# A hybrid decoder layer on one core: later uses of re-read left factors, and four factors of the output product in an earlier pair

## The chip, the cores and the metric

The program runs on one core of a Trainium2 chip. The metric is the device time of one execution in microseconds (us). The unchanged kernel took 1967.01 us as the median of 3 runs (1965.29 to 1967.56). Engines are named as in the profile: PE (TensorE matmul), PEld (its weight loads), DVE (VectorE), ACT (ScalarE), POOL (GpSimd), SP (SyncE, which issues the DMAs).

## The reference

One layer over 512 tokens of width 2048, all in float32: a normalised input projection, two kinds of attention heads side by side, an output projection with residual, and a gated feed-forward part with residual.

```python
h = rms_norm(x, norm1_g)
proj = h @ w_in                                     # 2048 x 6160
qa, ka, va, ra, ga, qb, kb, vb = split(proj)
log_g = log_sigmoid(ga @ gla_gate_w2 + gla_gate_b) / 16
out_a = rms_norm(chunked_gated_linear_attention(qa, ka, va, log_g)) * silu(ra)   # 4 heads
out_b = dilated_attention(rms_norm(qb), rms_norm(kb), vb, rel_bias)              # 8 heads
x = x + concat(out_a, out_b) @ w_out                # 2048 x 2048
h2 = rms_norm(x, norm2_g)
x = x + (silu(h2 @ w_gate) * (h2 @ w_up)) @ w_down  # 2048 x 5632, 5632 x 2048
```

## The kernel before, in words

**Products.** Every large product is done in pairs of 512 output columns. A pair halves the tokens, the contraction rows and the columns, and forms the 2 x 2 block product with seven block products (P1, P5, P6, P3, P7, P2, P4 in this order, line 32) in place of eight. Each of the seven has a left factor made of the activations (A11, S1, S2, S4, S3, A12, A22, line 37) and a right factor that is a quarter of the weights or the difference of two. With A21 for the fourth part, S1 = A21 + A22, S2 = S1 - A11, S4 = A12 - S2 and S3 = A11 - A21. The contraction is cut into four *groups* of 256 rows in each part, so a pair is 28 groups (21 in the last two pairs): group 0 to 3 are P1, 4 to 7 P5, 8 to 11 P6, 12 to 15 P3, 16 to 19 P7, 20 to 23 P2, 24 to 27 P4. "S1 of part 2" below means the factor S1 of the third 256-row cut; it is needed by group 6 of its pair.

**Precision.** Each factor is split in a high and a low float32r part, and a group is twelve 128x512 matmuls: eight with the high part of the weights (`wh`), four with the low part (`wl`).

**The stream.** `stream` (L318) runs over all groups of all pairs. In group k it emits, in this order: `run_soon`; a demand that the left factor of group k+1 exists (`ensure`, which calls `finish`); the ACT cast to `wh` of group k+1 (L331); the DVE difference of the weights of group k+2 where the product has one (L256; P5, P6, P7 and P4 do); the DVE difference that makes `wl` of group k+1 (L335); eight matmuls; a `step` of the background work; four matmuls. `wh` and `wl` have two buffers each.

**Background work.** Everything else is generators in the list `background`. `step(n)` takes n units from the head of the list (a `yield` is one unit unless it says another cost); each pair has its rate of units in a group. `later(units, fn)` runs fn some steps on, `soon(fn, groups)` some groups on, and `finish` draws from the head until a demanded factor is there.

**Left factors.** An activation block that ends a pair is transposed by PE, stored to DRAM (`transposed_store`, L1122), and read back in parts of 256 KB. `Operand.split` (L172) makes a factor of a part: an ACT cast (L174) and a DVE subtraction (L175), and for S1, S2, S4 and S3 a DVE addition or subtraction before (L1251, L1253, L1255 in `late_jobs`; L193 to L200 in `build`; L215 in `early`).

**The order of pairs.** The first pair (q, k of the linear attention) has an order written out by hand. Then follow the other input columns; the **sixth pair** is the gate `ra` (`final_gate`, L1155), under which the last dilated heads run as background. The **seventh and eighth pair** are the output projection, whose left factors (`opm`) come from the DRAM blocks `mix_d`: 4 to 7 from the dilated heads, 0 to 3 from the gate's four results. `final_out` (L1346) adds the residual, stores rows to `x1_d` and, in the eighth pair, writes the scaled and transposed blocks `xn_d` 4 to 7 of the next operand. `first_columns` (L1389) re-reads the rows that the seventh pair stored, scales and transposes them to `xn_d` 0 to 3; it runs in the eighth pair, as do `operand_jobs` (L1285, all factors of parts 0 and 1 of `opn`). The **ninth pair** is the first of eleven feed-forward pairs on `opn`; the last six pairs are the down projection.

**What sets the order on an engine.** The first pair is issued as written. For all the rest a planner in the framework orders each engine's instructions when the program is built. It keeps a simulated clock: the emission order is only a priority, and an instruction goes to its engine as soon as, by that clock, its inputs are there and nothing earlier in emission is ready. The engine then runs the planned order strictly, whatever the real times are.

Of the kernel before, what the change touches and what calls it, by code (L numbers as in the profile page):

```python
# [10 lines left out]
F32 = mybir.dt.float32  # L11
# [7 lines left out]
P = 128  # L19
# [88 lines left out]
def block_kernel(ctx: ExitStack, tc: tile.TileContext, ins, out):  # L108
# [56 lines left out]
    class Operand:  # L165
# [14 lines left out]
        def build(self, g, r11, r21, r12, r22):  # L180

            get = lambda r: r() if callable(r) else r
            tt = nc.vector.tensor_tensor
            r11, r22 = get(r11), get(r22)
            yield
            yield
            self.split("A11", g, r11)
            r21 = get(r21)
            yield
            self.split("A22", g, r22)  # L190
            r12 = get(r12)
            yield
            tt(r22, r21, r22, op=ALU.add)  # L193
            self.split("S1", g, r22)
            yield
            tt(r21, r11, r21, op=ALU.subtract)
            tt(r11, r22, r11, op=ALU.subtract)
            self.split("S2", g, r11)
            yield
            tt(r11, r12, r11, op=ALU.subtract)  # L200
            self.split("S4", g, r11)
            yield
            self.split("S3", g, r21)
            yield
            self.split("A12", g, r12)
            yield

        def early(self, g, r11, r21):

            pair_ = apool.tile([P, 2, 2, 256], F32, name=nm("top"), tag="A")  # L210
            r11, r21 = r11(pair_[:, 0]), r21(pair_[:, 1])
            yield
            self.split("A11", g, r11)
            yield
            nc.vector.tensor_tensor(r21, r11, r21, op=ALU.subtract)  # L215
            self.split("S3", g, r21)
            yield

# [99 lines left out]
    def stream(pairs):  # L318
# [183 lines left out]
    deferred = []  # L502

# [4 lines left out]
    def step(n=1):  # L508
        for d in list(deferred):
            d[0] -= 1  # L510
            if d[0] <= 0:
                deferred.remove(d)
                d[1]()
        if any(d[2] for d in deferred):
            return
        spent, cost = 0.0, 0
        while background and spent + 1e-6 < n:
            if spent:
                run_soon()
            try:  # L520
                cost = next(background[0])
                spent += 1.0 if cost is None else cost
            except StopIteration:
                background.pop(0)
        return spent

    def finish(ready):

        tries = 0
        while not ready():  # L530
            tries += 1
            assert tries < 100
            run_soon()
            try:
                next(background[0])
            except StopIteration:
                background.pop(0)
# [513 lines left out]
    def together(*gens):  # L1051

        gens = list(gens)
        while gens:
            spent = 0.0
            for g in list(gens):
                try:
                    cost = next(g)
                    spent += 1.0 if cost is None else cost
                except StopIteration:  # L1060
                    gens.remove(g)
            yield spent
# [8 lines left out]
    def heads_norm(t, then):  # L1071
# [8 lines left out]
        def rest():  # L1080
# [74 lines left out]
    def final_gate(half, which, tiles, acc_):  # L1155
        og = onorm.pop((half, which))
        if tiles is None:
            tiles = [cpool.tile([P, 512], F32, name=nm("cr"), tag="C") for _ in range(2)]
            src = acc_
        else:  # L1160
            src = tiles
        for m in range(2):
            if src is acc_:
                nc.vector.scalar_tensor_tensor(
                    halves(og[m]), unfolded(src[m]), row_scale(half, m), halves(og[m]),
                    op0=ALU.mult, op1=ALU.mult,
                )
                neg = nrs1[:, 2 * half + m : 2 * half + m + 1]
                nc.scalar.activation(halves(tiles[m]), unfolded(src[m]), AF.Exp, scale=neg)
            else:  # L1170
                nc.vector.tensor_tensor(og[m], src[m], og[m], op=ALU.mult)
                nc.scalar.activation(tiles[m], src[m], AF.Exp, scale=-1.0)
            nc.scalar.activation(tiles[m], tiles[m], AF.Ln, bias=1.0)
            nc.scalar.activation(tiles[m], tiles[m], AF.Exp, scale=-1.0)

        def rest():
# [3 lines left out]
            later(1 + (src is tiles), lambda: transposed_store(  # L1180
# [3 lines left out]
        soon(rest, 2)  # L1184
# [3 lines left out]
    def part(src, half):  # L1188
        def get(t=None):
            assert (id(src), half) in done  # L1190
            if t is None:
                t = rpool.tile([P, 2, 256], F32, name=nm("r"), tag="r")
            load(t, src[:, :, half * 256 : (half + 1) * 256])
            return t

        return get

    def early_jobs(op, groups, tops, flip):

        h0, h1 = (1, 0) if flip else (0, 1)  # L1200
        jobs = [op.early(g, part(tops[g], h0), part(tops[g], h1)) for g in groups]
        next(jobs[0])
        yield
        for i, job in enumerate(jobs):
            if i + 1 < len(jobs):
                next(jobs[i + 1])
# [402 lines left out]
```

## Time and profile before

| | |
|---|---|
| median of 3 runs | 1967.01 us (1965.29 to 1967.56) |
| the profiled execution's own time | 1968.84 us |
| its span, first to last instruction | 1967.1 us |
| PE busy | 1927.6 us (98%) |
| DVE busy | 1653.7 us (84%) |
| ACT busy | 1093.8 us (56%) |
| mean granted TensorE clock | 0.998 |

The busy shares are averages over the whole span. Where stretches are looked at one by one, a row gives the length, then the busy time of PE, PEld, DVE, ACT and POOL with the number of instructions in brackets, the granted clock and the share of the DMA engines. In the lists of waits a row reads: engine and line that waited, what it waited for, then us in total, how often, the longest. In a timeline a row is start, length, engine, line, what is written from what, how many, and in square brackets the idle time just before it with what ended it.

By the first matmul of each group of twelve, the sixth pair runs from 449.6 to 561.0 us, the seventh to 645.5, the eighth to 732.2, the ninth to 813.6 and the tenth to 887.9.

### The profile page before, as it was taken

To read this page: it belongs to the slowest core of one execution; us is meant where nothing else is said; L and a number is where in the kernel's file an instruction comes from. 1 tells how busy PE (TensorE), PEld (TensorE's weight loads), DVE (VectorE), ACT (ScalarE), POOL (GpSimd) and SP (SyncE) were. 2 spreads that over 40 slices of the span, in tenths; PEclk is the share of its full clock that TensorE was granted. 3 is DMA by queue.
4 is the path that set the end of the run, shared out by engine and by line. 5 is a ranking of instruction groups with operands and counts; after the bars stand their busy time and mean duration, and the time that the engine had idled before them with its cause. 6 is when DMAs were issued, how large, how long until landed. Compare 5 with 4: busy or idle time off the path is not lost.

```text
span 1967.1 us, 25785 instructions
## 1 busy us (share of the span) xinstructions
PE 1927.6 (98%) x9226; PEld 1670.9 (85%) x9226; DVE 1653.7 (84%) x1850; ACT 1093.8 (56%) x1600; POOL 60.9 (3%) x81
## 2 busy tenths in 40 slices
PE   8999999999999999999999999999999999999998
PEld 7888888888878877888888888888888888888887
DVE  8997787868789889878878878878879989989987
ACT  8554564566766766545545445545446646546443
POOL 0000230010000000000000000000000000000000
PEclk9999999999999999999999999999999999999999
DMA  8447455463766684554554553554555865855662
GB/s 278 141 162 266 119 171 170 134 200 124 221 213 202 215 288 152 177 167 133 178 170 127 179 163 127 176 164 130 172 163 168 299 203 185 310 183 175 236 214 75
DMA packets 237114, 360.45 MB, mean 183 GB/s; under 512 B 18246, under 2 KB 96783, under 8 KB 236984
## 3 DMA queue, kind: packets, MB, share of 16 engines
q1 hardware_dynamic: 236776, 358.72, 57.6%
q8 instruction: 72, 1.18, 0.3%
q14 instruction: 58, 0.48, 0.1%
q10 hardware_dynamic: 208, 0.08, 0.0%
HBM read 296.59 MB, written 64.51 MB: 184 GB/s over the span
## 4 chain that ended last, share of the span: by engine, by line
PE 75%; DVE 8%; DMA 5%; issue 3%; ACT 2%; POOL 0%; SPq 0%; DVEq 0%; ACTq 0%
PE acc L367 71%; DVE wl L335 3%; DVE wa L256 2%; PE bank L1129 1%; DVE AS L175 1%; PE bank L987 1%; DMA q<-in_x 1%; DMA xn_d<-oT 1%; ACT wh L331 1%; DMA q<-y_d 0%; DVE seed L294 0%; PE bank L1019 0%; DVE seed L1334 0%; DMA r<-xn_d 0%; DMA wc<-in_w_down 0%
## 5 line engine op out<-in xcount | busy, mean ns | idle before, releaser
L367 PE MATMUL acc<-wh,AS 128*128 128x512 f32 x3008 | 712.5, 380 | 0.6 <-ACT wh L331 0.5
L367 PEld LDWEIGHTS acc<-wh,AS 128*128 128x128 f32 x3008 | 569.8, 190 | 82.3 <-ACT wh L331 1.8
L331 ACT CAST wh<-wa 128x1024 fp32r<-128x1024 f32 x376 | 394.0, 1048 | 392.4 <-PE acc L367 363.0
L367 PE MATMUL acc<-wh,AA 128*128 128x512 f32 x2256 | 535.0, 380 | 0.0
L335 DVE TENSOR_TENSOR wl<-wa,wh 128x1024 fp32r<-128x1024 f32 x376 | 456.3, 1217 | 69.2 <-ACT wh L331 43.6
L367 PEld LDWEIGHTS acc<-wh,AA 128*128 128x128 f32 x2256 | 427.4, 190 | 61.4 <-ACT wh L331 0.9
L367 PE MATMUL acc<-wl,AS 128*128 128x512 f32 x1504 | 395.3, 385 | 9.7 <-DVE wl L335 9.5
L367 PEld LDWEIGHTS acc<-wl,AS 128*128 128x128 f32 x1504 | 279.4, 189 | 62.0 <-DVE wl L335 21.0
L367 PE MATMUL acc<-wl,AA 128*128 128x512 f32 x1128 | 298.1, 387 | 7.9 <-DVE wl L335 7.7
L367 PEld LDWEIGHTS acc<-wl,AA 128*128 128x128 f32 x1128 | 209.6, 190 | 41.5 <-DVE wl L335 12.4
L331 ACT CAST wh<-wb 128x1024 fp32r<-128x1024 f32 x94 | 98.5, 1049 | 129.7 <-PE acc L367 127.8
L331 ACT CAST wh<-wc 128x1024 fp32r<-128x1024 f32 x94 | 98.4, 1047 | 111.5 <-PE acc L367 101.7
L331 ACT CAST wh<-wd 128x1024 fp32r<-128x1024 f32 x94 | 98.5, 1048 | 105.8 <-PE acc L367 102.3
L256 DVE TENSOR_TENSOR wa<-wc,wa 128x1024 f32<-128x1024 f32 x94 | 114.4, 1221 | 46.2 <-DMA wc<-in_w_gate 25.1
L335 DVE TENSOR_TENSOR wl<-wc,wh 128x1024 fp32r<-128x1024 f32 x94 | 114.5, 1218 | 35.6 <-ACT wh L331 35.6
L335 DVE TENSOR_TENSOR wl<-wd,wh 128x1024 fp32r<-128x1024 f32 x94 | 114.3, 1219 | 34.9 <-ACT wh L331 28.2
L335 DVE TENSOR_TENSOR wl<-wb,wh 128x1024 fp32r<-128x1024 f32 x94 | 113.6, 1216 | 5.5 <-ACT wh L331 5.5
L256 DVE TENSOR_TENSOR wb<-wd,wb 128x1024 f32<-128x1024 f32 x94 | 114.3, 1216 | 1.1 <-DMA wd<-in_w_in 0.6
L256 DVE TENSOR_TENSOR wa<-wb,wa 128x1024 f32<-128x1024 f32 x94 | 113.6, 1218 | 0.8
L256 DVE TENSOR_TENSOR wa<-wd,wa 128x1024 f32<-128x1024 f32 x94 | 112.8, 1215 | 0.1
L298 DVE SCALAR_TENSOR_TENSOR seed<-acc,rs,seed 128x512 f32<-128x512 f32 x96 | 70.4, 745 | 24.9 <-PE acc L367 24.9
L282 ACT ACTIVATE seed<-acc,rs 128x512 f32<-128x512 f32 x96 | 60.6, 681 | 1.4 <-PE acc L367 0.8
(303 smaller groups left out, 1365.1 us busy)
## 6 DMA issues: line engine op xcount, KB each, us to landing
wa<-in_w_gate SPq DMA_DIRECT2D x44, 512.0 KB, 3.9
wb<-in_w_up SPq DMA_DIRECT2D x44, 512.0 KB, 4.3
wd<-in_w_up SPq DMA_DIRECT2D x44, 512.0 KB, 4.3
wc<-in_w_gate SPq DMA_DIRECT2D x44, 512.0 KB, 3.7
wc<-in_w_in SPq DMA_DIRECT2D x28, 512.0 KB, 3.9
wa<-in_w_in SPq DMA_DIRECT2D x24, 512.0 KB, 5.1
wb<-in_w_in SPq DMA_DIRECT2D x24, 512.0 KB, 6.0
wd<-in_w_in SPq DMA_DIRECT2D x24, 512.0 KB, 5.9
```

The lines of the kernel that those rows point to most:

```text
L175: nc.vector.tensor_tensor(a[:, :, 1, :], src, a[:, :, 0, :].bitcast(F32), op=ALU.subtract)
L256: nc.vector.tensor_tensor(src, self.quarter(one, g), src, op=ALU.subtract)
L282: nc.scalar.activation(halves(t), unfolded(src[m]), AF.Copy, scale=self.scale(half, m))
L298: nc.vector.scalar_tensor_tensor(halves(seed[m]), unfolded(src[m]), self.scale(half, m), halves(seed[m]), op0=ALU.mult, op1=ALU.add,)
L331: nc.scalar.copy(high[k], sources[k])
L335: nc.vector.tensor_tensor(low[k], sources.pop(k), high[k].bitcast(F32), op=ALU.subtract)
L367: nc.tensor.matmul(p.dst[prod][m], a[:, jj, hl, m * P : (m + 1) * P], folded(w[:, jj, :]), start=fresh and g == 0 and len(terms) == 2 and ...
L987: nc.tensor.matmul(lp[:, :n], qh[:, b * P : (b + 1) * P], kh[:, :n], start=True, stop=True)
L1129: nc.tensor.transpose(bk[:, jj, m * P : (m + 1) * P], tiles[m][:, f : f + P], ident)
```

## The change

1. **Three groups between a load and its use.** The stream keeps its group number in `now`. Generators may answer "wait" (`WAIT`, no unit spent), and `step` then asks the next generator in the list. The queue of loaded parts (`staged`) now holds the group of each load, and a use is emitted only when three groups have gone by (`ripe`), unless a factor is demanded (`hurry`). `early_jobs`, `late_jobs`, `operand_jobs` and the loops of `down_jobs` all go through it; `first_columns` waits in the same way between reading rows and scaling them.
2. **Four factors earlier.** S1 and S2 of parts 0 and 1 of `opm` leave the seventh pair's list and become `late_opm[0]`, which runs beside heads 6 and 7 of the dilated attention in the sixth pair, with tiles of its own from the large pool.
3. **The last result of a pair.** `final_gate` first copies the last product out of PSUM with ACT (`emitted`), and does the gate three groups on, where before DVE and ACT read PSUM at once. In the eighth pair's last result the scaling and the transposes come four steps later.
4. `operand_jobs` loads the four parts of part 1 into work tiles (`v`, `T`, `qT`, `kT`) in place of the small pool.

The core of the diff (the removed `build` and `early` are the functions named above):

```diff
@@ stream @@
+            now[0] = k
             run_soon()
             ensure(min(k + 1, last))
@@ background @@
+    now, hurry = [0], [False]
+    WAIT = -1.0
+    def advance():
+        i = 0
+        while i < len(background):
+            try:
+                cost = next(background[i])
+            except StopIteration:
+                background.pop(i)
+                continue
+            if cost is None or cost >= 0:
+                return 1.0 if cost is None else cost
+            i += 1
+        return None
+    def ripe(when):
+        return hurry[0] or now[0] >= when + 3
     def finish(ready):
-        tries = 0
         while not ready():
-            ...
+            hurry[0] = True
             run_soon()
+            assert advance() is not None
+        hurry[0] = False
@@ "qb1" @@
-            together(dil_heads(6), put_off(2, early_jobs(opm, (2,), mix_d[4:], True))),
+            together(dil_heads(6), put_off(2, early_jobs(opm, (2,), mix_d[4:], True)), late_opm[0]),
             early_jobs(opm, (3,), mix_d[4:], True),
-            late_jobs(opm, ((0, 1), (2, 3)), mix_d[4:], [mix_d[b] for b in order], True, 6),
+            late_opm[1],
@@ final_gate @@
+        last = tiles is None
+        if last:
+            tiles = emitted(acc_, lambda m: row_scale(half, m))
+        def gate():
+            for m in range(2):
+                nc.vector.tensor_tensor(og[m], tiles[m], og[m], op=ALU.mult)
+                nc.scalar.activation(tiles[m], tiles[m], AF.Exp, scale=-1.0)
+                nc.scalar.activation(tiles[m], tiles[m], AF.Ln, bias=1.0)
+                nc.scalar.activation(tiles[m], tiles[m], AF.Exp, scale=-1.0)
+            soon(rest, 2)
...
+        if last:
+            soon(gate, 3)
+        else:
+            gate()
@@ staged @@
+    def staged(items, ahead=1, cost=1.0):
+        queue = []
+        for keys, fetch, use in items:
+            while len(queue) > ahead or not all(key in done for key in keys):
+                if queue and ripe(queue[0][2]):
+                    t, u, when = queue.pop(0)
+                    u(t)
+                    yield cost
+                else:
+                    yield WAIT
+            queue.append((fetch(), use, now[0]))
...
@@ late_jobs @@
+        return staged(first_two(sooner, True), 1), rest
...
+    late_opm = late_jobs(
+        opm, ((2, 3),), mix_d[4:], [mix_d[b] for b in order], True, 6, sooner=(0, 1)
+    )
@@ final_out @@
-                turn = scaled_store(tiles, rows, tok, xn_d[2 * ch : 2 * ch + 2], 4 * ch)
...
+                def scaled():
+                    turn = scaled_store(tiles, rows, tok, xn_d[2 * ch : 2 * ch + 2], 4 * ch)
+                    later(2, turn)
+                if last:
+                    later(4, scaled)
+                else:
+                    scaled()
@@ first_columns @@
-        tiles = fetch(0)
-        yield
-        yield
+        tiles, when = fetch(0), now[0]
         for i, (ch, tok) in enumerate(places):
+            while not ripe(when):
+                yield WAIT
```

More of the change, by code (lines that the diff above doesn't have):

```diff
@@ L1275, in late_jobs @@
[L1275 to L1292 removed]
+                if own:
+                    spare[g] = apool.tile([P, 2, 2, 256], F32, name=nm("late"), tag="A")
+                    sums[g] = part_load(spare[g][:, 0], bots[g], h1)
+                    return part_load(spare[g][:, 1], tops[g], h1)
@@ new lines, in get, with other, first_two @@
+                t = rpool.tile([P, 2, 256], F32, name=nm("r"), tag="r")
+                sums[g] = part_load(t, bots[g], h1)
+                return fetch()
+            return [(id(bots[g]), h1)] + keys, get
+        def other(g, own):
+            keys, fetch = fetch_part(tops[g], h0, bufs)
+            if own:
+                return keys, lambda: part_load(spare[g][:, 1], tops[g], h0)
+            return keys, fetch
+        def first_two(part_, own):
+            return [(*both(g, own), sum_of("S1", g)) for g in part_] + [
+                (*other(g, own), sum_of("S2", g)) for g in part_
+            ]
@@ new lines, in late_jobs @@
+        items = [i for part_ in groups for i in first_two(part_, False)]
+        both_parts = list(sooner) + [g for part_ in groups for g in part_]
+        for g in both_parts:
+            items.append((*fetch_part(bots[g], h0, bufs), sum_of("S4", g)))
+        for name, half in (("A12", h0), ("A22", h1)):
+            for g in both_parts:
+                items.append((
+                    *fetch_part(bots[g], half, bufs), lambda t, name=name, g=g: op.split(name, g, t)
+                ))
@@ L1410, in first_columns @@
             if i < 3:
[L1411 removed]
+                tiles, when = fetch(i + 1), now[0]
             yield
```

232 lines of the change are left out of this document (92 added, 140 removed).

## The prediction

> **What bounds the kernel now.** I read the totals first, then the chain that ended last, then stretches of one pair each, then the waits inside the stretches that lose time. Totals, and a piece of the chain of waits in order of time (start, length, what):
>
> ```profile
> span 1967.1 us, 25785 instructions
> PE 1927.6 (98%) x9226; PEld 1670.9 (85%) x9226; DVE 1653.7 (84%) x1850; ACT 1093.8 (56%) x1600; POOL 60.9 (3%) x81
> ...
> 895.86 62.18 PE acc L367 x288
> ```
>
> PE bounds the whole: 288 matmuls in 62.18 us are 0.216 us each, so a group of twelve takes 2.59 us, and a pair of 28 groups 72.6. PE is idle for 39.5 us of 1967.1. The pairs six to ten, a row each, and then stretches inside the sixth, seventh and ninth:
>
> ```profile
> 449.60:561.00 111.40, 107.64 (x591) 93.28 (x590) 84.84 (x144) 76.35 (x163) 3.62 (x4) 1.00 0.60 188
> 561.00:645.50 84.50, 77.54 (x345) 64.86 (x344) 82.31 (x96) 52.46 (x78) 0.00 (x0) 0.98 0.62 202
> 645.50:732.20 86.70, 81.36 (x393) 68.53 (x392) 72.92 (x83) 61.05 (x104) 2.96 (x2) 1.00 0.73 237
> 732.20:813.60 81.40, 77.47 (x353) 65.88 (x353) 71.38 (x78) 48.37 (x66) 4.44 (x5) 0.98 0.61 186
> 813.60:887.90 74.30, 74.30 (x353) 65.08 (x352) 60.22 (x59) 37.12 (x43) 0.00 (x0) 1.00 0.52 160
> ...
> 519.00:561.00 42.00, 39.59 (x223) 34.07 (x222) 28.94 (x60) 29.97 (x63) 0.00 (x0) 1.00 0.82 259
> ...
> 561.00:602.00 41.00, 34.04 (x144) 26.83 (x143) 39.79 (x48) 25.70 (x38) 0.00 (x0) 0.96 0.43 136
> 602.00:645.50 43.50, 43.50 (x203) 38.03 (x202) 42.51 (x49) 26.76 (x41) 0.00 (x0) 1.00 0.79 265
> ...
> 732.20:766.00 33.80, 29.89 (x130) 24.42 (x130) 31.44 (x39) 24.37 (x40) 4.44 (x5) 0.95 0.58 187
> ```
>
> The tenth pair, 74.3 us, is a pair without trouble. The ninth does the same work in 81.4, and the seventh needs 84.5 where 345 matmuls would take 74.5. The seventh pair's loss lies in its first 41 us: PE 34.0 busy, DVE 39.8. DVE bounds there, with 1.2 us to spare; after 602 PE is full. In the last 42 us of the sixth pair DVE is busy for 28.9 only. So the loss that the change can reach is of two kinds: too much DVE work in a crowded stretch, and DVE or ACT standing before a load that is not there. The waits in three windows, from 563, 722 and 741 us on:
>
> ```profile
> PEld acc L367 <- DVE wl L335: 7.8, 7, 1.8
> PE acc L367 <- DVE wl L335: 4.9, 6, 1.4
> ACT AA L174 <- DMA top<-mix_d: 3.7, 1, 3.7
> ...
> PE bank L1129 <- DVE cr L1178: 2.0, 2, 1.8
> ...
> DVE top L215 <- DMA top<-xn_d: 4.8, 1, 4.8
> ...
> DVE r L1251 <- DMA r<-xn_d: 1.9, 1, 1.9
> ```
>
> PE mostly waits for `wl`, and `wl` stands behind S-factors and behind waits for `top` and `r`.
>
> **How far emission reaches.** DVE in the timeline at the start of the seventh pair:
>
> ```profile
> 562.17 1.23 DVE L256 TENSOR_TENSOR wa<-wb,wa 128x1024 f32<-128x1024 f32 x1
> 563.43 1.23 DVE L256 TENSOR_TENSOR wb<-wd,wb 128x1024 f32<-128x1024 f32 x1
> ...
> 565.71 0.69 DVE L175 TENSOR_TENSOR AA<-top,AA 128x512 fp32r<-128x512 f32 x1
> 566.31 0.69 DVE L215 TENSOR_TENSOR top<-top 128x512 f32<-128x512 f32 x1
> 566.91 1.41 DVE L1164 SCALAR_TENSOR_TENSOR og<-acc,rs,og 128x512 f32<-128x512 f32 x2
> ```
>
> `wb<-wd,wb` is the weight difference of P7 group 0, emitted in group 14, and it runs in group 0 or 1: the planner fills any hole with whatever it takes for ready, thirteen groups ahead. So emission three groups later is no delay by itself. It only lets the stream's own work go first where both are ready, which matters on the crowded DVE and little on ACT. Three short operations in a row start 0.60 us apart (565.71, 566.31, 566.91), so I count 0.6 us for each addition, subtraction or split half on DVE.
>
> **The change, term by term.**
>
> *Four factors moved.* S1 and S2 of parts 0 and 1 are eight DVE operations and four casts. Before, the two S1 sums still ran in the sixth pair (the second at 560.31, in the row below); six operations ran in the crowded 41 us: 6 x 0.6 = 3.6 us, one for one on the path as DVE bounds there. I take -3.6; the other end is 0, if the planner fills the room with other work of low priority.
>
> ```profile
> 560.31 0.69 DVE L1251 TENSOR_TENSOR r<-T,r 128x512 f32<-128x512 f32 x1 [2.61 <-DMA r<-mix_d]
> ...
> L174 ACT CAST AS<-r 128x512 fp32r<-128x512 f32 x11 | 6.7, 622 | 5.8 <-DVE r L1253 2.4 <-DVE r L1255 2.2 <-DVE r L1251 1.2
> ```
>
> Their price in the sixth pair: 8 x 0.6 = 4.8 us of DVE and 4 x 0.62 = 2.5 of ACT, in 42 us where DVE has 13.1 free and ACT 12.0. Cover is this idle time; but a softmax operation that PE's transposes wait for can come behind a factor. Ends 0 and +4.8; +0.5 is taken, near the free end because of that room. Six more loads of 256 KB go to SP there instead of in the seventh pair, where DMA is at 0.43 against 0.82; that falls under the same ends.
>
> *Uses behind their loads, seventh pair.* The cast of A11 of part 3 stood 3.7 us before its load. ACT is idle in the plan, so I expect it to be planned where it was; what can go is DVE's spare 1.2 us. Ends -1.2 and 0, taken -0.6. S1 of part 2 is emitted in group 2 (before: 3), S4 of part 3 in group 9 (before: 10), so the eight S-factors of parts 2 and 3 still crowd groups 2 to 9.
>
> *The last gate result.* ACT gets two PSUM copies of 0.6 to 0.7 us, DVE two plain products for the two of 1.41 us in all; ACT has 15 us free in that stretch. Zero, with ends of 1.4 either way. Its stores come in group 5 (before: 2), the first use, S4 of part 2, is needed by group 14. The PE wait for `cr`, 2.0 us, may go, but DVE is the bound beneath it.
>
> *First columns, eighth pair.* Chunk by chunk: before, scaled in groups 1, 2, 4, 5 and stored in 3, 5, 6, 8; now 3, 6, 9, 12 and 6, 9, 12, 13.
>
> ```profile
> ACT L L1342 <- POOL prox L159: 3.8, 1, 3.8
> ...
> PE bank L1129 <- ACT L L1342: 1.4, 2, 1.1
> ```
>
> The 3.8 us before POOL I leave as it is; the transposes come behind stream matmuls, which saves between 0 and 1.4: -0.7. What is late next: A11 of part 0 of the ninth pair's operand is emitted in group 14 (before: 10), the last of part 1 in group 26 (23). All are needed from group 28 on.
>
> *End of the eighth and start of the ninth pair.* Before, A11 and S3 of part 2 are emitted in group 25 and 26 behind loads of group 24, and S1 of part 2 in group 27 with its load. Now the loads come in group 27, A11 of parts 2 and 3 is demanded in groups 1 and 2 of the ninth pair, S1 follows in 2, S2 in 4 and 7, S4 in 13 and 14 on demand (before: 4 and 7). PE in the timeline, and two links of the chain:
>
> ```profile
> 731.26 0.91 PE L367 MATMUL acc<-wl,AA 128*128 128x512 f32 x3 [1.97 <-DVE wl L335]
> ...
> 747.24 1.72 PE L367 MATMUL acc<-wl,AA 128*128 128x512 f32 x4 [2.36 <-DVE wl L335]
> 748.75 3.04 PE L367 MATMUL acc<-wh,AS 128*128 128x512 f32 x8
> ...
> 735.56 4.46 DMA xn_d<-oT
> ...
> 740.03 4.59 DMA r<-xn_d
> ```
>
> S1's load lands at 744.6; PE wants S1 of part 2 in group 6, some 732.2 + 6 x 2.59 = 747.7 us. The load is in time, only `wl` must not stand behind it. What can go: 1.97 + 2.36, and the slow eight matmuls after the second gap, 3.04 against 8 x 0.216 = 1.73, so 1.3: together 5.6. The other end is 0 without new collisions (those are a rival below). I take half, -2.8: DVE work pushed here from earlier groups fills some of the freed 4.8 + 1.9 us.
>
> PE's clock falls after such gaps:
>
> ```profile
> 573.05 0.44 PE L1129 MATMUL bank<-mats,cr 128*128 128x128 f32 x2 [1.81 <-DVE cr L1178]
> 574.84 3.02 PE L367 MATMUL acc<-wh,AA 128*128 128x512 f32 x8
> ```
>
> Here an idle gap of 1.81 us stands before eight matmuls in 3.02 us. The Trainium skill, "TensorE: Matmul & The Clock Gate" (Part 1: The HAM clock gate), says that the array goes to half clock after at least one idle window of about 3.4 us. By that rule gaps of 2 us would not do it and the slow matmuls would stay whatever the change does: the sum would lose half of 1.3 us and be -6.5 in place of -7.2. The trace does not agree, with 1.81 and 2.36 us before the two slow stretches.
>
> *Feed-forward and down pairs.* The uses of `down_jobs` begin three groups later, still one in a group; the first factor is demanded some twenty groups after it is made. Zero; ends of 0.5 either way.
>
> Sum: -3.6 + 0.5 - 0.6 - 0.7 - 2.8 = -7.2 us. The profiled span 1967.1 becomes 1959.9. The profiled execution took 1968.84, which is 1.8 over the median of 1967.01; the span happens to equal the median, so I give 1960.
>
> **Rivals.**
>
> *The distance is empty.* The planner puts every use where it put it before, and only the moved factors count: -3.6 + 0.5, so 1964. For it: the P7 row above. Against it: DVE is at 97% in the seventh pair's start, where priority decides. A measurement of this kernel can tell some 0.2%, 3.9 us; this would count as no change.
>
> *Slower: late factors meet P4's weight differences.* In the eighth pair the weight differences of P4 are emitted in groups 22 to 25. A22, S1, S2 and S4 of part 1, eight DVE operations, move from groups 19 to 21, which have none, to 22 to 24; A11 of parts 2 and 3 and S3 of part 2, four operations, move to the ninth pair's first groups. If no idle time of DVE takes them, 12 x 0.6 = 7.2 us fall on PE's path: 1967.1 + 7.2 - 3.6 + 0.5 = 1971. It decides from 3.1 us on, when the gain of the moved factors is eaten. Against it: DVE has 86.7 - 72.9 = 13.8 us idle in that pair.
>
> *More than forecast.* All waits before loads go: 1.2 in the seventh, 1.4 in the eighth, 1.97 at its end and the ninth pair at the tenth's 74.3 instead of 81.4: 3.6 + 1.2 + 1.4 + 2.0 + 7.1 = 15.3, so 1952. Against it: the ninth pair still has a dozen factor operations more to do on DVE than the tenth.
>
> **How the numbers follow.** Forecast (1956 to 1963) 0.42; empty distance 0.20; slower 0.18; more 0.18; anything else 0.02. Faster is the forecast, the third rival and a little of the first: 0.63; the rest of the first is within 0.2%: 0.19; slower 0.18. The range goes from a little beyond the third rival to the second: 1951 to 1971. The likeliest case alone has 1956 to 1963.
>
> **What would show it.** Seventh pair near 80 us with six fewer DVE operations in its first part; the sixth no longer than 112; L1251 for `opm` parts 0 and 1 well before the pair ends; no `top<-xn_d` wait of DVE over 2 us; the ninth near 78. A sixth pair of 114 or an eighth of 90 would make it wrong, as would softmax waits (L1012 on L1003) growing by more than 3 us.

## The result and the profile after

The changed kernel took 1971.96 us, the median of 7 runs (1970.0 to 1975.35), against 1967.12 us for 7 runs of the kernel before: ratio 1.0027, 95% interval 1.0015 to 1.0038. It is slower by 0.1 to 0.4% where 0.4% faster was forecast. The profiled execution took 1971.96 us, its span is 1969.9 us.

The totals after:

```profile
span 1969.9 us, 25756 instructions
PE 1930.8 (98%) x9226; PEld 1668.1 (85%) x9226; DVE 1653.7 (84%) x1850; ACT 1095.8 (56%) x1602; POOL 62.0 (3%) x81
```

The work is the same (9226 matmuls, 1850 operations of DVE); two more ACT operations are the copies out of PSUM. So the difference lies in waits and in the clock. The pairs six to ten of the kernel after, then its nineteenth pair (the last feed-forward pair), and stretches of the sixth and seventh; columns as before:

```profile
450.10:562.40 112.30, 108.92 (x591) 93.95 (x589) 89.52 (x149) 77.12 (x166) 3.65 (x4) 0.98 0.58 186
562.40:648.10 85.70, 77.40 (x345) 64.96 (x344) 77.62 (x90) 52.52 (x78) 0.00 (x0) 0.96 0.61 200
648.10:734.90 86.80, 81.69 (x393) 68.25 (x392) 71.10 (x80) 60.82 (x103) 2.97 (x2) 1.00 0.71 236
734.90:814.70 79.80, 76.40 (x353) 64.79 (x354) 72.75 (x80) 49.33 (x68) 6.08 (x5) 1.00 0.61 189
814.70:889.10 74.40, 74.40 (x353) 64.89 (x352) 60.10 (x59) 37.09 (x43) 0.00 (x0) 1.00 0.52 160
1484.50:1561.90 77.40, 76.59 (x354) 64.20 (x353) 74.98 (x86) 51.20 (x70) 0.00 (x0) 1.00 0.68 222
...
562.40:603.40 41.00, 32.70 (x139) 26.24 (x138) 35.25 (x43) 25.35 (x38) 0.00 (x0) 0.92 0.44 143
```

The nineteenth pair before, for comparison:

```profile
1482.70:1557.70 75.00, 74.95 (x353) 64.91 (x352) 74.66 (x86) 50.85 (x70) 0.00 (x0) 1.00 0.71 230
```

Pair by pair, after less before: sixth +0.9, seventh +1.2, eighth +0.1, ninth -1.6, nineteenth +2.4. The move did take DVE work out of the seventh pair: 82.31 us became 77.62, and 39.8 became 35.25 in its first 41 us. But PE is busy for 32.70 us there and was for 34.04, and the clock fell from 0.96 to 0.92. The waits of the seventh pair show where PE stands:

```profile
PEld acc L329 <- DVE wl L296: 10.9, 8, 5.4
...
PE acc L329 <- DVE wl L296: 8.3, 6, 5.0
...
DVE top L1204 <- DMA top<-mix_d: 4.9, 1, 4.9
```

And the timeline of that place (SPq is the queue that issues the DMAs):

```profile
559.18 0.34 SPq L1012 DMA_DIRECT2D mix_d<-r  x1
...
566.33 1.18 SPq L1166 DMA_DIRECT2D top<-mix_d  x2
...
570.56 0.69 DVE L1204 TENSOR_TENSOR top<-top 128x512 f32<-128x512 f32 x1 [4.94 <-DMA top<-mix_d]
571.17 0.68 DVE L175 TENSOR_TENSOR AS<-late,AS 128x512 fp32r<-128x512 f32 x1
...
572.63 0.69 DVE L1143 TENSOR_TENSOR og<-cout,og 128x512 f32<-128x512 f32 x1 [0.78 <-DMA og<-ong_d]
573.24 1.22 DVE L296 TENSOR_TENSOR wl<-wa,wh 128x1024 fp32r<-128x1024 f32 x1
...
574.51 2.07 PE L329 MATMUL acc<-wl,AA 128*128 128x512 f32 x4 [5.05 <-DVE wl L296]
...
576.38 3.01 PE L329 MATMUL acc<-wh,AA 128*128 128x512 f32 x8
```

The load of the last `top` block waits in its queue for head 7's store (6.8 us). That store is issued at 559.18, the load at 566.33, and DVE gets the block at 570.56: 11.4 us, which three groups (3 x 2.59 = 7.8 us) do not cover. DVE stands idle for 4.94 us with a `wl` queued behind, PE stands for 5.05 us, and then runs slowly (eight matmuls in 3.01 us, 1.73 at full clock).

In the sixth pair there is a second such place, on ACT (here `kT` is a key block of a dilated head):

```profile
509.04 0.33 SPq L1012 DMA_DIRECT2D mix_d<-r  x1
...
512.41 0.68 ACT L956 ACTIVATE k<-bank,gk 128x512 f32<-128x512 f32 x1
...
513.94 1.18 SPq L1166 DMA_DIRECT2D top<-mix_d  x2
...
514.58 0.60 PE L955 MATMUL bank<-mats,kT 128*128 128x128 f32 x4
...
516.15 1.28 DVE L1143 TENSOR_TENSOR og<-seed,og 128x512 f32<-128x512 f32 x2
...
517.17 0.62 ACT L174 CAST AA<-top 128x512 fp32r<-128x512 f32 x1 [4.08 <-DMA top<-mix_d]
517.69 1.04 ACT L292 CAST wh<-wb 128x1024 fp32r<-128x1024 f32 x1
...
518.64 0.68 ACT L956 ACTIVATE qT<-bank,gq 128x512 f32<-128x512 f32 x1
...
519.22 0.68 ACT L956 ACTIVATE kT<-bank,gk 128x512 f32<-128x512 f32 x1
...
519.95 0.49 PE L964 MATMUL bank<-kT,qT 128*128 128x128 f32 x2 [1.96 <-ACT kT L956]
...
520.18 1.14 ACT L1144 ACTIVATE seed<-seed 128x512 f32<-128x512 f32 x2
...
522.93 2.44 PE L329 MATMUL acc<-wh,AS 128*128 128x512 f32 x8
```

ACT stands for 4.08 us before the cast of a `top` block. The casts to `qT` and `kT` of a head, whose inputs PE has made by 515.2 us, are queued behind it; PE waits 1.96 us for them and then runs slowly (eight matmuls in 2.44 us).

### The profile page after: what moved, and what is told of

Same layout as the page of the kernel before. It is cut to its first block, busy times and chain, and to the rows that moved or that the text cites. A ratio compares the mean times of both kernels' runs of the same rounds, so it can differ in the third digit from the quotient of the medians.

```text
span 1969.9 us, 25756 instructions
## 1 busy us (share of the span) xinstructions
PE 1930.8 (98%) x9226; PEld 1668.1 (85%) x9226; DVE 1653.7 (84%) x1850; ACT 1095.8 (56%) x1602; POOL 62.0 (3%) x81
## 4 chain that ended last, share of the span: by engine, by line
PE 81%; DVE 9%; DMA 4%; issue 3%; ACT 2%; POOL 1%; SPq 0%; DVEq 0%; ACTq 0%; POOLq 0%
PE acc L329 73%; DVE wl L296 3%; PE acc L397 3%; DVE wa L217 2%; PE bank L1109 1%; DVE AS L175 1%; PE bank L964 1%; DMA k<-in_x 1%; PE bank L996 0%; ACT wh L292 0%; DMA q<-in_x 0%; PE bank L749 0%; DMA mix_d<-r 0%; PE bank L989 0%; ACT jk L1057 0%
## 5 line engine op out<-in xcount | busy, mean ns | idle before, releaser
L292 ACT CAST wh<-wc 128x1024 fp32r<-128x1024 f32 x94 | 98.5, 1047 | 114.1 <-PE acc L329 102.6
```

Source lines behind the costliest of these rows:

```text
L292: nc.scalar.copy(high[k], sources[k])
```

## The experiments

Each ratio is to the kernel before, measured beside it on the same chip. Lengths of pairs are from one profiled execution each, and the sixth pair of one and the same kernel differs by 2 to 3.5 us between two executions (before 111.4 and 109.3, after 112.3 and 115.8); times are therefore read from the medians and profiles are used for the place. The runs come from five chips; the text says where two kernels that it compares ran on one.

**How wide a ratio of equal kernels is.** The kernel before and the changed kernel, each once more, on another chip.

> The kernel before, unchanged, under another name: how far a ratio of equal kernels goes from 1. Expected 0.9995 to 1.0005; if it goes further, the ratios of the other runs are to be read with that width.

1967.13 us, ratio 0.9999 (0.9991 to 1.0008).

> The changed kernel, unchanged, beside the first two on the same chip. Expected ratio 1.002 to 1.0035, seventh pair 84 to 87 us with a wait of VectorE on top of 2 to 7 us, nineteenth 76.5 to 78.

1968.43 us, ratio 1.0012 (1.0003 to 1.0020), below the ratio expected. Seventh pair 83.4 us, VectorE's wait 3.6, nineteenth 76.5. The change costs 0.12% here and 0.27% on the first chip; a difference of 0.1% between kernels of different chips carries nothing.

**The move alone.** The kernel before with S1 and S2 of parts 0 and 1 beside heads 6 and 7, everything else as it was:

```diff
-            together(dil_heads(6), put_off(2, early_jobs(opm, (2,), mix_d[4:], True))),
+            together(dil_heads(6), put_off(2, early_jobs(opm, (2,), mix_d[4:], True)), late_opm[0]),
-            late_jobs(opm, ((0, 1), (2, 3)), mix_d[4:], [mix_d[b] for b in order], True, 6),
+            late_opm[1],
```

> The kernel before with only the four factors moved: S1 and S2 of parts 0 and 1 made beside heads 6 and 7 in the sixth pair, in tiles of their own; no distance, old gate, old first columns. Theory C: DVE busy in the seventh pair falls by 4 to 5 us, idle time before a load takes its place, and the time is 1965 to 1972. Theory D: 1963 to 1964, the 3.1 us of the forecast.

1964.19 us, ratio 0.9987 (0.9978 to 0.9995): 3.3 us below the 1967.46 beside it. Forecast for these terms: -3.1. The place is another: seventh pair -2.1, eighth -2.1 in its profile.

**The rest without the move.** The changed kernel with the four factors back in the seventh pair's list (the diff above reversed, `late_opm` made of both groups).

> The changed kernel with S1 and S2 of parts 0 and 1 back in the seventh pair's list; all else as changed. Theory C (moving the four factors took 4 to 5 us of DVE work out of the seventh pair, but DVE then came earlier to the difference on the last top part and stood there, so nothing was gained): DVE busy in the seventh pair rises from 77.6 to about 82 us, its wait before top falls from 4.9 us to under 2, and the time is within 3 us of 1972. Theory D (the move gains its 3.6 us and something else loses): the time rises to 1975 or more.

1969.54 us, ratio 1.0013 (1.0004 to 1.0022). So the move wins 0.13% on the old emission, and the rest loses 0.13% by itself. The two do not add up to the changed kernel (1.0027 and 1.0012): within the new emission the move is not seen to win. DVE's wait before `top` in the seventh pair is gone here, as was expected.

**No distance.** The changed kernel with

```diff
-        return hurry[0] or now[0] >= when + 3
+        return hurry[0] or now[0] >= when
```

> The changed kernel with the distance of three groups set to zero (a use is emitted as soon as its turn comes); all else as changed. Theory A (the planner places a use where its simulated clock has the load landed, whatever the emission): the waits of DVE and ACT before re-read parts stay at 30 to 40 us in all (before 35.1, changed 36.2), and the time stays within 4 us of the changed kernel's 1972. Theory B (emission distance sets the order, and late emission costs): the eighth and ninth pair and the eleventh feed-forward pair change by several us together, and the time falls to 1967 or below.

1976.3 us, ratio 1.0048 (1.0036 to 1.0061), sixth pair 117.4, eighth 90.0. The waits of DVE and ACT on re-read parts are 24.6 us (30 to 40 were expected). The distance isn't empty, and it is not what makes the new code slow: without it the kernel is no faster (the chip is another than that of 1.0027). It follows that this kernel is not the kernel before with the move: the rewritten queues order the work differently even at distance zero.

**Uses held back.** The changed kernel, each use tied behind the last emitted cast to `wh` and the last `wl`, so that the planner can't place it ahead of them:

```diff
-                    u(t)
+                    with tc.issue_after(recent["act"]), tc.issue_after(recent["dve"]):
+                        u(t)
```

> The changed kernel, and every use of a re-read part is tied behind the stream's wh cast and wl difference that were emitted last before it, so that the planner can't place it earlier; emission, loads and work are as changed. Theory A: the distance becomes real, the waits of DVE and ACT before re-read parts fall from 36 us to under 12, the seventh pair loses its 4.9 us wait and falls from 85.7 to about 80, and the time falls by 5 to 10 us, to 1962 to 1967. Theory B: the waits weren't the loss, and the time stays at 1970 to 1975 or rises, since uses are later still.

1971.22 us, ratio 1.0022 (1.0013 to 1.0031). The waits of ACT and DVE on re-read parts fall from 36.2 us in 17 places to 2.5 in 2, and the time stays near that of the changed kernel. That does not show that the waits cost nothing. The sixth pair falls to 108.6 us and the seventh to 83.0, but the ninth grows to 83.8, where ACT waits 5.0 us for a POOL operation that is slow in this kernel and in two others (last section). The changed kernel has no such wait, and its ninth pair is 79.8; without the 4 us between them (an estimate from these two lengths) this kernel would lie near 1967 us, at the edge of what Theory A names. Which of the two theories holds stays open.

**The same hold on the move alone.** The kernel of the move, with the sixth pair's uses tied in this way.

> The kernel before with the four factors moved as in the run of that alone, and the uses of re-read parts in the sixth pair (A11, S3 and the four moved factors) tied behind the stream's cast and difference emitted last before them. Theory A, for this place: holding took the sixth pair to 108.6 us where everything was held; here too the sixth pair falls from 111.4 to under 110, nothing later is made late, and the time is 1961 to 1963. Rival: the heads' chain and not the loads sets that pair, and the time is 1964 or more.

1965.68 us, ratio 0.9981 (0.9972 to 0.9989): not told apart from the move alone, on another chip. The sixth pair did not fall in its profile (114.1 us), so the rival's time came, and whether the heads' chain is the reason is not shown.

**The late factors behind the heads.** The changed kernel with `late_opm[0]` listed after both pairs of heads and the last early job, not beside heads 6 and 7.

```diff
-            together(dil_heads(6), put_off(2, early_jobs(opm, (2,), mix_d[4:], True)), late_opm[0]),
+            together(dil_heads(6), put_off(2, early_jobs(opm, (2,), mix_d[4:], True))),
             early_jobs(opm, (3,), mix_d[4:], True),
+            late_opm[0],
```

> The changed kernel with the four moved factors behind the last two heads in the list of background work instead of beside them. Theory F (beside the heads they hold up the store of head 7, which landed at 566.3 against 557.7 without the move, and so the last top part, before which DVE stands 4.9 us): the store lands 4 us or more earlier, the wait before top falls below 2.5 us, the seventh pair goes from 85.7 to about 82, and the time falls by 3 to 4 us, to 1968. Rival: the store is late for another reason (ACT's gate work in front of it), the wait stays and the time stays at 1971 to 1973.

1970.01 us, ratio 1.0009 (1.0000 to 1.0019). VectorE's wait on the last block is 2.0 us, the seventh pair 84.3. The wait fell as Theory F says, the pair by 1.4 us where 3.7 were expected, and the time lies between the two forecasts: it decides nothing.

**The down factors.** First the changed kernel with no distance in `down_jobs` alone (`ripe(when, far)`, far = 0 there); then the kernel before with three empty groups ahead of the first use.

> The changed kernel with the distance taken away from the down projection's factors alone (their uses are emitted as in the kernel before). Theory E (the three empty groups at the start of that list push three factors into crowded groups of the last feed-forward pair): that pair goes back from 77.4 to 75.0 us and the time falls by some 2 us, to 1970. Rival: the 2.4 us of that pair are chance of one profile, and the time stays within 1 us of 1972.

1972.28 us, ratio 1.0018 (1.0009 to 1.0026): not the 1970 of Theory E. The nineteenth pair is back at 75.00, in this row of that kernel, but its seventh is 87.3, with a wait of VectorE on `top` of 7.0 us:

```profile
1487.20:1562.20 75.00, 74.95 (x354) 64.83 (x353) 74.65 (x86) 51.10 (x70) 0.00 (x0) 1.00 0.69 231
```

> The kernel before with one thing alone: three groups pass between the first loads of the down projection's parts and their first use. Theory E: the last feed-forward pair grows from 75.0 to 77 us, and the time rises by about 2 us, to 1969. Rival: no change, 1967.

1966.72 us, ratio 0.9988 (0.9980 to 0.9997), nineteenth 75.0. One delay at the start does no harm. Why this kernel has a ratio as low as the move alone (0.9987) was not followed up; the kernel before has its highest median, 1968.89, on this chip, and a gain of 0.1% in a single kernel is weak evidence. The new code spaces every factor by three groups with at most four loads in flight; all eight kernels with that have a nineteenth pair of 76.1 to 77.9 us, the twelve others 75.0.

**The eighth pair onward, and its complement.** In the first kernel the output product's factors and the last gate result are emitted by the old code, with the move; distances lie from the eighth pair on. The second is the reverse: the new code up to the seventh pair, the old one behind. The diffs exchange whole functions (`early_jobs`, `late_jobs`, `final_gate`; `first_columns`, `operand_jobs`, `final_out`, `down_jobs`) against those of the kernel before.

> The changed kernel, but for the operand of the output product: its factors are loaded and used as before the change (a use stands one unit behind its load), the last gate result is emitted as before, and only the four late factors are moved. What is left of the distances lies from the eighth pair on. Theory A (the distances in the sixth and seventh pairs cost what the move wins, since vector subtractions of the weights then stand behind a subtraction that waits for a row block): the seventh pair falls to about 82.5 us as with the move alone, the ninth stays near 80, the nineteenth stays near 77; ratio 0.998 to 1.000. Theory B (the distances cost it in the later pairs): seventh above 84.5 or the sum of the pairs behind the eighth 4 us above the move alone; ratio 1.001 to 1.003.

1964.9 us, ratio 0.9987 (0.9977 to 0.9997).

> The complement: the changed kernel up to the seventh pair, and everything of the second operand, the first columns and the down factors as before the change. Theory A: the seventh pair stays near 85.7 us and loses its half clock as in the changed kernel, the ninth is back near 81, the nineteenth at 75.0; ratio 1.000 to 1.002. Theory B: the seventh falls to 82.5, the ratio to 0.9985.

1970.48 us, ratio 1.0013 (1.0004 to 1.0021). The loss lies in the emission of the sixth and seventh pairs; the intervals do not meet, and both kernels ran on one chip. The seventh pair itself is 83.1 us in the first and 83.7 in the second, not the 85.7 expected there. The later pairs are exchanged the other way; in the profiles they make the second kernel 0.5 us longer in all (eighth +1.4, ninth +0.6, nineteenth -1.5).

**The old gate, and no distance for the down factors.** The changed kernel with the old `final_gate`; and the first kernel of the last paragraph with far = 0 in `down_jobs`.

> The changed kernel with the emission of the last gate result as before the change (no copy out of the accumulators, the gate at once). Theory G (the gate's three groups of distance, which put the product of the norm behind the load that the last head's store holds up, cost the seventh pair): seventh 83 us or less and no wait of VectorE over 2 us there; ratio 1.000 to 1.001. Against it (the gate is not the cause): seventh within 1 us of 85.7, ratio 1.002 to 1.004.

1971.68 us, ratio 1.0019 (1.0010 to 1.0027), seventh 85.5, VectorE's wait 3.8: the gate is not the cause.

> The kernel that keeps the old order in the sixth and seventh pairs and the move, with the distances of the eighth and ninth pairs but with the down factors used as soon as they are loaded. Theory A: seventh 82.5, ninth 80, nineteenth 75.0 us: 4 to 5 us below the kernel before, ratio 0.9975 to 0.998, the fastest of all. Theory B: not faster than the move alone (0.9987).

1965.03 us, ratio 0.9991 (0.9982 to 0.9999), against 0.9987 for the move alone, so the distances of the eighth and ninth pairs win nothing that can be measured. Nor does far = 0 here: the first kernel of the last paragraph, on the same chip, has 1964.9 us with a nineteenth pair of 76.5, this one 1965.03 with 75.0.

**The wait in the seventh pair taken away.** The changed kernel with the difference of the last `top` block emitted eight groups behind its load; and the same with far = 0 in `down_jobs`.

```diff
-            queue.append((fetch(), use, now[0]))
+            queue.append((fetch(), use, now[0] + getattr(use, "more", 0)))
...
+            differ.more = 5 if flip and groups == (3,) else 0
```

> The changed kernel, with one use moved: the difference of the last row block of the sixth and seventh pairs (top, group 3, whose weights are wanted only in the fifth of the seven products) is emitted eight groups behind its load, not three. Theory A (the loss of the seventh pair is the wait of VectorE on this load, with a weight's low half queued behind it): no wait of VectorE on top over 1 us in the seventh pair, its granted clock 0.99 or 1.00, its length 82 to 83.5 us for 85.7; ratio 1.000 to 1.002, 2 to 3 us below the changed kernel beside it. Rival (the weights are late for another reason): the wait goes, and the pair stays at 85 or more.

1968.92 us, ratio 1.0014 (1.0005 to 1.0023); the changed kernel beside it 1.0012. The waits of its seventh pair, and of ACT and PE in its sixth:

```profile
PE acc L329 <- DVE wl L296: 4.1, 4, 1.7
...
ACT AA L174 <- DMA top<-mix_d: 6.5, 2, 4.5
...
PE bank L964 <- ACT kT L956: 2.4, 1, 2.4
```

The wait of VectorE, 3.6 us in the changed kernel on this chip, is gone, PE's longest gap at `wl` is 1.7 us, and no time is won (seventh pair 84.2 us, 83.4 in the changed kernel). So this wait, the clearest in the profile, is not by itself the loss. The wait on ACT in the sixth pair is still there.

> The same edit, and the down factors used as soon as they are loaded. If the two places hold all of the loss: seventh 82 to 83.5, nineteenth 75.0 us, ratio 0.999 to 1.0005, so 4 to 5 us below the changed kernel. If a loss is left beside them: 1.001 or more.

1967.34 us, ratio 1.0003 (0.9994 to 1.0012), nineteenth 75.01: 1.6 us below the last kernel, near the 1.8 us that its nineteenth pair (76.8) is longer. The changed kernel is 1.1 us above, not 4 to 5; the two places together bring the kernel back to the one before, but not the gain of the move.

**Top tiles or late sums.** Both on the kernel that has the move, the old code in the sixth and seventh pairs and far = 0 (0.9991): in the first, only `early_jobs(opm, ...)` is the new function, in the second only `late_jobs(opm, ...)`.

> The kernel of e12 (move, old order in the sixth and seventh pairs, 0.9991), with the first factors and differences (top tiles) of the output product emitted three groups behind their loads as in the changed kernel. Theory A1 (the distance of the top tiles holds the loss): ratio 1.0005 to 1.002, a wait of VectorE on top in the seventh pair. Theory A2 (the distance of the late sums holds it): ratio 0.9985 to 0.9995, no such wait.

1973.78 us, ratio 1.0033 (1.0021 to 1.0045), above both theories' ranges; VectorE's wait on `top` in the seventh pair is 0.6 us.

> The kernel of e12, with the late sums and parts (late, r, v to PT tiles) of the output product emitted three groups behind their loads as in the changed kernel. Theory A1: ratio 0.9985 to 0.9995. Theory A2: ratio 1.0005 to 1.002. If both kernels lie between, near 1.000, the loss is shared.

1965.98 us, ratio 0.9997 (0.9988 to 1.0005). The new emission of the `top` tiles holds the loss: 7.8 us between the two kernels, on one chip. How much of it is a cost of `top` is less sure. Against the common base (0.9991, on another chip) the first kernel is some 8 us slower and the second some 1 us; both have a wait of ACT on POOL of 5 us that the base has not (last section), so by estimate the new `top` code costs some 3 us and the new code of the late sums wins some 4. The sixth pairs of the two, the first one's row first, each in its own profile:

```profile
450.10:566.30 116.20, 110.06 (x590) 94.97 (x589) 90.30 (x152) 78.83 (x169) 3.80 (x4) 0.97 0.59 189
```

```profile
450.90:561.60 110.70, 106.84 (x583) 92.36 (x583) 89.46 (x150) 77.27 (x166) 3.61 (x4) 1.00 0.61 198
```

and the waits on `top` there, in the same order:

```profile
ACT AA L174 <- DMA top<-mix_d: 8.1, 2, 5.5
...
PE bank L975 <- ACT kT L967: 3.8, 2, 3.4
```

```profile
ACT AA L174 <- DMA top<-mix_d: 3.4, 2, 2.5
...
PE bank L975 <- ACT kT L967: 0.3, 1, 0.3
```

This pattern divides all kernels. Leaving out the two with held uses, PE's longest wait on `kT` in the sixth pair is 2.0 to 3.4 us in the eleven with the new `top` code (the changed kernel twice) and 0.6 or less in the seven with the old code (the kernel before twice). The order on ACT differs. Here is the kernel with the old order at this place, to be read beside the timeline after:

```profile
511.47 1.65 SPq L1023 DMA_DIRECT2D mix_d<-r  x1
...
514.46 0.68 ACT L967 ACTIVATE k<-bank,gk 128x512 f32<-128x512 f32 x1
515.03 1.15 ACT L1163 ACTIVATE seed<-seed 128x512 f32<-128x512 f32 x2
516.07 1.14 ACT L1164 ACTIVATE seed<-seed 128x512 f32<-128x512 f32 x2
516.08 1.18 SPq L1346 DMA_DIRECT2D top<-mix_d  x2
...
517.11 1.14 ACT L1165 ACTIVATE seed<-seed 128x512 f32<-128x512 f32 x2
...
520.40 0.62 ACT L174 CAST AA<-top 128x512 fp32r<-128x512 f32 x1 [1.21 <-DMA top<-mix_d]
```

Here six activations of the gate fill the time until the block lands. In the new order they come after it (520.18 in the timeline after), but they could not have filled it there: DVE makes the product that they wait for only at 516.15 to 517.43. What has moved against the stream is the block. Counted by the first matmul of each group, head 5's last store is issued at the start of group 15 in all twelve kernels with the new `top` code (509.04 above) and around the start of group 16 in all eight with the old (511.47); the load follows, and the cast begins in group 17 in the eleven and in group 18 or 19 in the seven. So the uses did not come later here, they came about a group earlier, and ACT stood at the cast for 2.1 to 5.6 us (0.4 to 2.8 with the old code). By the code the old `early_jobs` spends three units of background work on parts 0 and 1, the new one two, and "wait" spends none, so that the heads listed beside it move on a unit sooner. That this is the reason was not tried by itself. The one with distance zero also casts in group 17 (its wait is 2.1 us, the one on `kT` 2.4), so the rewritten queue and not the distance makes it.

That this place is what the time pays for is argued, not shown. For it: a stretch of half clock, 3.4 or 6.8 us long, begins between 519 and 525 us in eight of the eleven and in none of the others. Against it: the length of the sixth pair does not divide the kernels, with 111.4 to 117.4 us in the eleven (mean 114.2) and 109.3 to 115.2 in the seven (mean 111.9), and no kernel changed this place alone. In the seventh pair, too, a change of emission moved DVE's waits; there the kernel with the last difference held back shows that its removal alone wins nothing.

## Why the prediction was wrong

The step that failed is the conclusion drawn under "How far emission reaches": that later emission "only lets the stream's own work go first", which matters "little on ACT", so that a cast would be "planned where it was". By it the sum has -0.6 us for the uses behind their loads and no term at all for what the new queues do in the sixth pair. The runs show a loss in its place: 5.6 us between the new and the old emission of the sixth and seventh pairs (1970.48 and 1964.9), with the new code of the `top` tiles in it (some 3 us by itself, by the estimate above). The casts were not planned where they were. That of part 3 began 7.0 us into the seventh pair, 3.2 before; that of part 2, in the sixth, ran about a group earlier, as did the heads that store its block, and ACT stood before it with two head casts queued behind. The prediction read the change as a delay of uses; it did not ask what a queue that spends fewer units does to the jobs listed beside it, nor what stands behind a waiting cast on ACT, which is busy for 56% only. How the 5.6 us arise from this, place by place, stays open. The sentence "emission three groups later is no delay by itself" is not what the runs refute: without the distance the new code is no faster.

- *Four factors moved*, -3.6 + 0.5: right in size, -3.3 us with the move alone. "One for one on the path" was not: DVE is as busy in the first 41 us of the seventh pair as before (39.86 us), filled by other work, PE is busy 37.45 for 34.04 there, and half of the gain appears in the eighth pair.

```profile
560.90:601.90 41.00, 37.45 (x184) 30.90 (x184) 39.86 (x48) 27.76 (x44) 0.00 (x0) 1.00 0.46 148
```

- *Uses behind their loads, seventh pair*, -0.6: wrong in sign and the main miss, and not in the seventh pair alone. The kernel with the new code of the `top` tiles is 7.8 us above the one with that of the late sums; the two kernels that part the change at the eighth pair give 5.6 us.
- *The last gate result*, 0: not contradicted (1.0019 with the old gate; the changed kernel was not run on that chip).
- *First columns*, -0.7: not seen. The eighth pair is 86.8 for 86.7, and ACT's 3.8 us before POOL stand as they were.
- *End of the eighth and ninth pair*, -2.8: the mechanism was right, the size half. VectorE's wait of 4.8 us on `top<-xn_d` is gone, the longest gap of PE in the first groups is 1.00 us (2.36 before), the clock is 1.00:

```profile
740.52 1.13 PE L329 MATMUL acc<-wl,AA 128*128 128x512 f32 x4 [1.00 <-DVE wl L296]
```

  Over eleven profiles with the new code the ninth pair has 79.8 us in the mean, over six with the old 80.9: -1.1. The three kernels with the slow POOL operation are left out; theirs is 83.8 to 85.4. The medians do not show it.
- *Feed-forward and down pairs*, 0 within 0.5: wrong by the profiles, where the nineteenth pair of the changed kernel pays 1.5 to 2.4 us. Of the two pairs of medians on one chip, one shows it (1.6 us) and one does not (-0.1 us). ACT's casts stand before loads of `S_d` there:

```profile
ACT AS L174 <- DMA v<-S_d: 3.6, 3, 1.5
ACT AS L174 <- DMA T<-S_d: 2.6, 2, 2.3
ACT AS L174 <- DMA qT<-S_d: 2.5, 1, 2.5
```

- *The clock.* In the sixth pair after, a PE gap of 1.96 us stands before slow matmuls, as 1.81 and 2.36 us did before. The rule of the Trainium skill, "TensorE: Matmul & The Clock Gate" (Part 1: The HAM clock gate), of at least one idle window of about 3.4 us, can be met by the gap of 5.05 us but not by this one; the trace decides.
- *The rivals.* The slower one named 1971 us and came near for another reason: its place, the eighth pair, is unchanged. The empty distance fell: the change is slower, and the kernel without the distance is another again.
- *What would show it.* Seventh near 80 (85.7), sixth at most 112 (112.3) and ninth near 78 (79.8) all failed in the first profile; the wait on `top<-xn_d` went, and the softmax waits did not grow (2.1 us before, 1.4 after).

The fastest kernels measured are the move alone, the move with the distances from the eighth pair on (0.9987 both) and the move with held uses (0.9981). All three have the move and the old emission up to the seventh pair; the kernel before with three empty groups ahead of the down factors measured 0.9988 as well.

## What to carry to other kernels

Distance between a load and its use has to be counted from when the load can be issued, and a load of a block just stored waits for that store: here 11.4 us from store to use, for 7.8 us of distance. When the accounting of background work changes, everything listed beside it moves too: ask where the jobs beside a rewritten one will run, and what will be queued behind a waiting use on its own engine, idle engines too. The largest wait in a profile need not hold the time: taking it away by itself, as was done here for the wait in the seventh pair, is the test.

## What the runs showed of the hardware

A POOL operation on 128x4 took 1.10 us in one kernel and 9.79 us in another, with the same order of instructions on DVE and ACT around it; the row of the first is from the kernel with the move, the old code in the sixth and seventh pairs and far = 0 in `down_jobs`, the others from the kernel with the new code of the late sums. The profile's spans on POOL are rough; the wait of ACT is not one of them:

```profile
739.18 1.10 POOL L158 TENSOR_SCALAR rs<-tmp 128x4 f32<-128x4 f32 x1 [83.05 <-DVE tmp L1596]
```

```profile
734.25 9.79 POOL L158 TENSOR_SCALAR rs<-tmp 128x4 f32<-128x4 f32 x1 [83.22 <-DVE tmp L1596]
...
746.68 1.26 ACT L254 ACTIVATE seed<-acc,rs 128x512 f32<-128x512 f32 x2 [5.01 <-POOL rs L1600]
```

ACT then stands for 5.0 us and the ninth pair takes 84.7 us for 79.6. Both kernels of the last pair of experiments have it (9.79 us each), and so has the one with all uses held (7.52); no other does. The two of the last pair pay it alike, so their difference stands, but each would be some 5 us faster without it by its profile (an estimate from 84.7 - 79.6). What makes POOL slow there was not tried.
